# The low part of the weight tiles in block 0: from GpSimd to VectorE

## The chip, the cores and the metric

One core of a Trainium2 chip. The metric is device time in microseconds (us) of one execution of the whole program, median of three runs: 2673.79 us for the kernel before (2673.79 to 2675.59).

## The reference, cut to what matters

One layer of a recurrent decoder with two branches that read the same normalised input: a gated linear recurrence (LRU) and a gated delta rule (GDN). 2048 prompt tokens and 8 x 8 sample tokens go through it, in float32:

```python
u = rms_norm(x, norm_pre)
z = einsum('btd,de->bte', u, w_in)            # 1024 x 8208
# z -> lru_x, lru_gate, q|k|v, gdn_gate, b, a, m_lru, m_gdn
lru_out = rg_lru(conv(lru_x)) * silu(lru_gate)
gdn_out = norm(gated_delta_rule(conv+silu(q|k|v), g, beta)) * silu(gdn_gate)
merged  = sigmoid(m_lru) * (lru_out @ w_br_lru) + sigmoid(m_gdn) * (gdn_out @ w_br_gdn)
x_new   = x + rms_norm(merged @ w_out, norm_post)
```

Every weight matrix is used for every token. There are also the states of both branches as outputs.

## The kernel before, in words

**Precision by splitting.** TensorE works on a rounded float32 type. Each operand of a large product is therefore kept as two tiles, hi (the value rounded) and lo (the value minus hi), and a product is three matmuls: hi by hi, hi by lo and lo by hi (lines 551, 553 and 555 in `proj`). `split` (line 203) makes such a pair: ScalarE writes hi with a copy (it is recorded under line 143, as everything that goes through the ordered ScalarE wrapper), and another engine subtracts (line 205). Which engine that is, is the last argument of `split`: GpSimd where none is given.

**Blocks.** The 2048 prompt tokens are worked in four blocks of 512; block 0 also carries the 64 sample tokens, so its products have 576 columns (a half of 256 and a half of 320). A block goes through the same steps: normalised input (`u_tile`), then eight heads' k projections with their Gram matrices and a batched triangular inverse (`t_gram`, `t_inv`), the LRU groups (`t_lru`), then for each head the q, v and gate projections with the recurrent chain (`t_q`, `t_v`, `t_samp`, `t_chain`), then the two branch products (`branch`) and the output product (line 1294 on).

**Weights.** They are used in a fixed order (`worder`), 88 tiles of 128 x 1024 for a block. In block 0 each tile is read raw from the inputs by SyncE's queue (`wload`, lines 260 to 271), split into hi and lo in one tile `whl` (`wfetch`, line 296), and the pair is written to a DRAM scratch `dW` (`wstore`, line 279). In blocks 1 to 3 the pair is read back from there (line 300) and no split is done. `whl` has three buffers, the raw tiles two or three. `wfetch` runs one tile ahead of its use, a raw tile is loaded one or two tiles before that, and a tile's store is handed to SyncE's queue one tile later than its split. So a buffer of `whl` comes free when its matmuls have read it and its store has landed; a raw buffer comes free when both halves of the split have read it, and the next raw load on SyncE's queue waits for that.

**Who sets the order.** TensorE runs in the order of the program text, in which `Weave` mixes small tasks into the long projections. On the other engines the framework orders the instructions by their place in the text and their readiness in its own schedule; each engine then works strictly in that order and waits at an instruction whose inputs are late. On ScalarE a wrapper (`Ordered`) makes every later ScalarE instruction of a projection follow the hi of the tile that was fetched just before.

**The line that is changed.** In `wfetch`, `out` is true for the eight tiles of the output weight (their raw tile is `rawo`), which are split by ScalarE and VectorE already; the other 80 tiles of block 0 (raw tiles `raw` and `raws`) are split by ScalarE and GpSimd:

```python
wlast[0] = split(hi, lo, wraws[key(e)], V if out else None)
```

VectorE's other work in block 0 that the prediction speaks of: the convolution (lines 582 and 588, whose two tensor inputs both lie in SBUF), the elementwise part of SiLU (597), the inverse (816 to 826), the chain (1061, 1072, 1076), and the lo halves of activations (`xl` in `t_lru`, `bt` in the branch stage).

Of the kernel before, what the change touches and what calls it, by code (L numbers as in the profile page):

```python
# [154 lines left out]
def body(ctx, tc, x_prompt, x_sample, state_lru_conv, state_lru_h, state_gdn_conv, state_gdn_S,  # L155
# [5 lines left out]
    V, T, SP = nc.vector, nc.tensor, nc.sync  # L161
# [41 lines left out]
    def split(hi, lo, src, eng=None):  # L203
        r = A.activation(hi, src, AF.Copy)
        (eng or G).tensor_tensor(out=lo, in0=src, in1=hi.bitcast(F32), op=OP.subtract)  # L205
        return r
# [28 lines left out]
    key = lambda e: (e[0].tensor.name, e[1])  # L235
# [4 lines left out]
    wstores, wraws = [], {}  # L240

    wready = []
    wlast = [None]
# [3 lines left out]
    def wtile():  # L247
        ring[0] += 1
        if wx and ring[0] % 4 == 0:
            return wx[0].tile([128, 2, 1024], F32R, name="whx", tag="whx")  # L250
        return wp.tile([128, 2, 1024], F32R, name="whl", tag="whl", bufs=3)

    def wload(n):

        src, c = e = worder[n]
        if key(e) in wraws:
            return
        if isinstance(c, tuple):
            raw = rw.tile([128, 4, 256], F32, name="rawo", tag="raws")
            SP.dma_start(raw, src[c[1] * 512:(c[1] + 1) * 512, c[0] * 256:(c[0] + 1) * 256]  # L260
                         .rearrange("(k p) c -> p k c", p=128))
            wraws[key(e)] = raw
        elif not (paired[0] <= n < paired[1] or paired[2] <= n < paired[3]):
            raw = rw.tile([128, 8, 128], F32, name="raws", tag="raws")
            SP.dma_start(raw, src[:, c:c + 128].rearrange("(k p) c -> p k c", p=128))
            wraws[key(e)] = raw
        else:
            two = [key(x) for x in worder[n:n + 7]].count((src.tensor.name, c + 128))
            w = 128 + 128 * two
            raw = rp[0].tile([128, 8, w], F32, name="raw", tag="raw")  # L270
            SP.dma_start(raw, src[:, c:c + w].rearrange("(k p) c -> p k c", p=128))
            for j in range(1 + two):
                wraws[src.tensor.name, c + 128 * j] = raw[:, :, 128 * j:128 * j + 128]

    def wstore(held=0):

        while len(wstores) > held:
            i, hl = wstores.pop(0)
            SP.dma_start(dW[i], hl.bitcast(F32))

    def wfetch(ahead):

        while wnext[0] < len(worder) and len(wready) < ahead:
            n = wnext[0]
            e = worder[n]
            place = wplace[key(e)]
            out = isinstance(e[1], tuple)
            hl = wtile()
            hi, lo = (hl[:, j].rearrange("p (k c) -> p k c", c=256 if out else 128) for j in range(2))
            if n < len(wplace):  # L290
                while lnext[0] < len(wplace) and lnext[0] <= n + (
                        2 if paired[0] <= lnext[0] < paired[1] else 1):
                    wload(lnext[0])
                    lnext[0] += 1
                wstore(1)
                wlast[0] = split(hi, lo, wraws[key(e)], V if out else None)
                wstores.append((place, hl))
            else:
                wstore()
                SP.dma_start(hl.bitcast(F32), dW[place])  # L300
            wready.append((hi, lo))
            wnext[0] += 1

    def nextw():
        wfetch(1)
        w = wready.pop(0)
        return w
# [104 lines left out]
    with tc.tile_pool(name="init", bufs=2, side="right") as ip:  # L412
        with tc.tile_pool(name="u0", bufs=1) as up:
            r0 = ip.tile([8, 128], F32, name="r0")
            SP.dma_start(r0, rows(norm_pre))
            xh = u_load(0, up)
            t = gtile()
            tr(t[:, :8], r0, ident[:8, :8])
            V.tensor_copy(npre, t[:, :8])
            wraw = ip.tile([128, 8, 16], F32, name="wraw", bufs=1)  # L420
            SP.dma_start(wraw, win[:, C_B:C_B + 16].rearrange("(k p) c -> p k c", p=128))
            u_norm(xh, up)
            for n in range(2):
                wload(n)
                lnext[0] += 1
            SP.dma_start(dtb, bass.AP(tensor=gdn_dt_bias.tensor, offset=gdn_dt_bias.offset, ap=[[0, 128], [1, 8]]))
            SP.dma_start(negA, bass.AP(tensor=gdn_A_log.tensor, offset=gdn_A_log.offset, ap=[[0, 128], [1, 8]]))
            u = [u_tile(xh, k) for k in range(8)]
            zz = ip.tile([128, 96], F32, name="zz", bufs=1)
            V.memset(zz, 0.0)  # L430
            V.tensor_copy(wst[:, 256:352], zz)
            V.tensor_copy(wst3[:, :, 0:16], wraw)
            V.tensor_tensor(out=wst3[:, :, 16:32], in0=wraw, in1=wst3[:, :, 0:16].bitcast(F32), op=OP.subtract)
            wfetch(2)
# [96 lines left out]
    for blkno in range(NBLK):  # L531
# [9 lines left out]
        def proj(mov, evac):  # L541
            w = nextw()
            wfetch(3 if blkno else 1)
            A.after = wlast[0]
            hi, lo = w
            for c0, n in halves:
                ps = pmm.tile([128, 512], F32, name="mm", tag="mm")
                for k in range(8):
                    mh, ml = mov[k]
                    wh = hi[:, k, :]  # L550
                    T.matmul(ps[:, :n], wh, mh[:, c0:c0 + n], start=k == 0, stop=False)  # L551
                    W.pump(n * 0.4219)
                    T.matmul(ps[:, :n], wh, ml[:, c0:c0 + n], start=False, stop=False)  # L553
                    W.pump(n * 0.4219)
                    T.matmul(ps[:, :n], lo[:, k, :], mh[:, c0:c0 + n], start=False, stop=k == 7)  # L555
                    if k < 7:
                        W.pump(n * 0.4219)
                evac(ps, c0, n)
                W.pump(n * 0.4219)
# [654 lines left out]
        for k in range(8):  # L1214
            hi = pA.tile([128, TB + NS], F32R, name="a", tag="a")
            lo = pA.tile([128, TB + NS], F32R, name="a", tag="a")
# [20 lines left out]
        for dd in range(8):  # L1237
# [5 lines left out]
            hi = Bp.tile([128, NB], F32R, name="bt", tag="bt")  # L1243
            lo = Bp.tile([128, NB], F32R, name="bt", tag="bt")
# [108 lines left out]
```

## Time and profile before

| | before |
|---|---|
| median of three runs | 2673.79 us |
| the profiled execution | 2683.59 us, of which its span is 2681.9 us |
| TensorE busy (matmul) | 2571.7 us, 96% |
| VectorE busy | 1503.4 us, 56% |
| ScalarE busy | 885.4 us, 33% |
| GpSimd busy | 565.8 us, 21% |
| DMA | 581.82 MB, mean 217 GB/s |

The span runs from the first to the last instruction; the rest of the profiled execution lies around it. Busy shares are over the whole span. Block 0 ends near 886 us of it, the other three blocks take some 599 us each. In the rows PE is TensorE, DVE VectorE, ACT ScalarE, POOL GpSimd, SP SyncE; L205 is line 205; a name with q is an engine's queue. PEclk is the share of full clock that TensorE was granted.

### The profile page before, as it was taken

What the parts mean: (1) busy time and instruction counts of PE and PEld (TensorE: products, weight loads), DVE (VectorE), ACT (ScalarE), POOL (GpSimd) and SP (SyncE); (2) the same over time, 40 slices, a digit from 0 to 9 for tenths busy, and PEclk for the clock granted to TensorE, in tenths of its full rate; (3) what the DMA queues carried; (4) which work ended last, traced back from release to release, by engine and by line L of the source; (5) the groups of instructions that cost most, each with busy time, mean ns of one, the idle gap of its engine ahead of it and who ended that gap; (6) DMA issues with size and microseconds to landing.
All of it is one profiled execution on the core that took longest, in us unless ns stands there. A gap on an engine that the chain in (4) does not pass through costs nothing.

```text
span 2681.9 us, 39950 instructions
## 1 busy us (share of the span) xinstructions
PE 2571.7 (96%) x15332; PEld 2237.5 (83%) x15332; DVE 1503.4 (56%) x3441; ACT 885.4 (33%) x1722; POOL 565.8 (21%) x444
## 2 busy tenths in 40 slices
PE   6888799999999999999999999999999999999999
PEld 5887798888999788888889888888889888888888
DVE  4668477787434557566522557566513458566512
ACT  5324543333324225333302235333303235333301
POOL 2442342232540211100120121110210211110200
PEclk9988899999999999999999999999999999999999
DMA  7987978789887887554466787544466887555465
GB/s 190 250 257 187 228 207 187 203 176 179 255 292 256 283 277 222 200 177 158 154 237 256 260 283 225 203 163 163 154 245 256 270 272 217 200 172 168 160 236 200
DMA packets 327897, 581.82 MB, mean 217 GB/s; under 512 B 70849, under 2 KB 236762, under 8 KB 282650
## 3 DMA queue, kind: packets, MB, share of 16 engines
q1 hardware_dynamic: 313882, 553.57, 66.9%
q10 hardware_dynamic: 13824, 25.70, 2.5%
q8 instruction: 121, 1.98, 0.3%
q14 instruction: 70, 0.57, 0.1%
HBM read 421.61 MB, written 157.59 MB: 216 GB/s over the span
## 4 chain that ended last, share of the span: by engine, by line
PE 68%; DMA 3%; issue 2%; DVE 1%; POOL 1%; ACT 1%; SPq 0%; ACTq 0%; POOLq 0%; DVEq 0%
PE mm L555 17%; PE mm L551 16%; PE mm L553 16%; PE g L192 5%; PE c L192 4%; PE mm L1294 2%; PE mm L1298 2%; PE mm L1296 2%; PE g L196 2%; DMA er<-dgc 1%; DMA dgc<-gr 0%; DMA npb<-in_norm_post_dram 0%; DMA ux<-in_x_prompt_dram 0%; DMA whl<-dW 0%; POOL er L756 0%
## 5 line engine op out<-in xcount | busy, mean ns | idle before, releaser
L551 PE MATMUL mm<-a,whl 128*128 128x512 f32 (+2 forms) x2432 | 865.0, 356 | 25.2 <-ACT tmo L143 18.5
L555 PE MATMUL mm<-a,whl 128*128 128x512 f32 (+2 forms) x2432 | 869.6, 358 | 4.8 <-POOL whl L205 4.8
L553 PE MATMUL mm<-a,whl 128*128 128x512 f32 (+2 forms) x2432 | 863.9, 355 | 0.0
L551 PEld LDWEIGHTS mm<-a,whl 128*128 128x128 f32 x2432 | 466.7, 192 | 74.7 <-ACT tmo L143 20.0
L555 PEld LDWEIGHTS mm<-a,whl 128*128 128x128 f32 x2432 | 466.7, 192 | 58.0 <-POOL whl L205 5.4
L553 PEld LDWEIGHTS mm<-a,whl 128*128 128x128 f32 x2432 | 466.7, 192 | 45.6
L582 DVE SCALAR_TENSOR_TENSOR cvy<-cvr,cwg,cvy 128x512 f32<-128x512 f32 x288 | 224.7, 780 | 17.8 <-ACT cvy L143 12.4
L553 PE MATMUL mm<-a,whx 128*128 128x512 f32 x448 | 181.7, 406 | 0.0
L555 PE MATMUL mm<-a,whx 128*128 128x512 f32 x448 | 181.4, 405 | 0.0
L551 PE MATMUL mm<-a,whx 128*128 128x512 f32 x448 | 179.3, 400 | 0.0
L1232 DVE SCALAR_TENSOR_TENSOR pt<-tm,mm 128x512 f32<-128x512 f32 (+1 forms) x80 | 47.4, 592 | 189.8 <-PE mm L555 189.8
L143 ACT ACTIVATE cvr<-mm 128x512 f32<-128x512 f32 (+1 forms) x160 | 81.7, 510 | 175.4 <-PE mm L555 167.3
L1086 POOL TENSOR_TENSOR st<-st,mhalf 128x4 f32<-128x4 f32 x32 | 32.3, 1009 | 507.8 <-DVE st L1084 496.0
L205 POOL TENSOR_TENSOR whl<-raw,whl 128x1024 fp32r<-128x1024 f32 x44 | 108.8, 2474 | 118.4 <-ACT whl L143 108.6
L205 POOL TENSOR_TENSOR whl<-raws,whl 128x1024 fp32r<-128x1024 f32 x36 | 89.8, 2495 | 188.6 <-ACT whl L143 176.5
L1296 PE MATMUL mm<-whl,bt 128*128 128x256 f32 x448 | 126.4, 282 | 0.8 <-DVE whl L205 0.8
L1294 PE MATMUL mm<-whl,bt 128*128 128x256 f32 x448 | 126.2, 282 | 0.8 <-DVE y L1303 0.8
L1298 PE MATMUL mm<-whl,bt 128*128 128x256 f32 x448 | 126.2, 282 | 0.6 <-DVE yss L1272 0.6
L143 ACT ACTIVATE th<-cvy 128x512 f32<-128x512 f32 (+1 forms) x96 | 61.9, 644 | 195.7 <-DVE cvy L582 128.6
L143 ACT ACTIVATE yv<-c 128x128 f32<-128x128 f32 x128 | 35.5, 278 | 243.7 <-PE c L192 243.2
L555 PE MATMUL mm<-gp,whl 128*128 128x512 f32 (+2 forms) x296 | 104.2, 352 | 0.0
L551 PE MATMUL mm<-gp,whl 128*128 128x512 f32 (+2 forms) x296 | 104.1, 352 | 0.0
(341 smaller groups left out, 4637.8 us busy)
## 6 DMA issues: line engine op xcount, KB each, us to landing
whl<-dW SPq DMA_DIRECT2D x199, 1024.0 KB
dW<-whl SPq DMA_DIRECT2D x88, 1024.0 KB
whx<-dW SPq DMA_DIRECT2D x65, 1024.0 KB
raws<-in_w_in_dram SPq DMA_DIRECT2D x33, 512.0 KB
raw<-in_w_in_dram SPq DMA_DIRECT2D x15, 1024.0 KB
dtm<-tmo ACTq DMA_DIRECT2D x48, 256.0 KB
tm<-dtm SPq DMA_DIRECT2D x48, 256.0 KB
ux<-in_x_prompt_dram SPq DMA_DIRECT2D x16, 512.0 KB
```

The costliest lines, as they stand in the source:

```text
L143: r = f(*args, **kw)
L192: T.matmul(out, a, b, start=start, stop=stop)
L196: T.transpose(out, in_, idn)
L205: (eng or G).tensor_tensor(out=lo, in0=src, in1=hi.bitcast(F32), op=OP.subtract)
L551: T.matmul(ps[:, :n], wh, mh[:, c0:c0 + n], start=k == 0, stop=False)
L553: T.matmul(ps[:, :n], wh, ml[:, c0:c0 + n], start=False, stop=False)
L555: T.matmul(ps[:, :n], lo[:, k, :], mh[:, c0:c0 + n], start=False, stop=k == 7)
L582: V.scalar_tensor_tensor(out=y[:, :TB], in0=raw[:, i:i + TB], scalar=cw[:, i, ti:ti + 1], in1=y[:, :TB], op0=OP.mult, op1=OP.add)
L1232: proj(mov, lambda ps, c0, n: V.scalar_tensor_tensor(out=t_[:, c0:c0 + n], in0=x[:, c0:c0 + n], scalar=1.0, in1=ps[:, :n], op0=OP.add, op1 ...
L1294: T.matmul(ps[:, :256], mh[:, cs], wh[:, k % 4], start=k == 0, stop=False)
L1296: T.matmul(ps[:, :256], mh[:, cs], wl[:, k % 4], start=False, stop=False)
L1298: T.matmul(ps[:, :256], ml[:, cs], wh[:, k % 4], start=False, stop=k == 7)
```

## The change

The subtraction that makes lo of a weight tile goes to VectorE for all 88 tiles of block 0. Nothing else is edited.

```diff
@@ wfetch @@
                 wstore(1)
-                wlast[0] = split(hi, lo, wraws[key(e)], V if out else None)
+                wlast[0] = split(hi, lo, wraws[key(e)], V)
                 wstores.append((place, hl))
```

## Rows read from the trace of the kernel before

**Rows 1.** Busy time by stretch of block 0 (us, engines, PEclk, DMA).

```profile
core 0: us, PE busy (x) PEld busy (x) DVE busy (x) ACT busy (x) POOL busy (x), PEclk, DMA share, GB/s
0.00:75.00 75.00, 49.76 (x314) 43.42 (x315) 34.87 (x112) 39.07 (x83) 20.28 (x24) 1.00 0.74 198
75.00:220.00 145.00, 122.34 (x836) 117.74 (x836) 89.18 (x247) 45.03 (x92) 64.19 (x48) 0.93 0.88 245
220.00:312.00 92.00, 65.65 (x407) 64.23 (x407) 65.93 (x171) 46.55 (x81) 28.74 (x18) 0.82 0.84 206
312.00:411.00 99.00, 93.55 (x685) 90.69 (x684) 69.34 (x140) 48.05 (x86) 40.43 (x23) 0.95 0.84 224
411.00:700.00 289.00, 272.46 (x2012) 242.62 (x2012) 219.19 (x526) 98.72 (x230) 82.24 (x47) 1.00 0.84 181
700.00:803.00 103.00, 103.00 (x778) 103.00 (x777) 35.07 (x46) 28.22 (x36) 60.22 (x31) 1.00 0.82 300
```

**Rows 2.** Waits of PE, 0 to 886 us (total us, times, longest).

```profile
PE mm L551 <- ACT tmo L143: 18.5, 6, 7.3
...
PE g L196 <- DVE cvy L597: 9.4, 7, 1.4
PE c L192 <- DVE S L1072: 6.8, 7, 1.3
...
PE mm L555 <- POOL whl L205: 4.8, 2, 2.9
```

**Rows 3.** Instructions of line 205 (ns min/median/max, first and last start us, forms).

```profile
L205 POOL TENSOR_TENSOR whl<-raw,whl x44: 2340/2400/3160, 61.6 to 799.0; 128x1024 fp32r<-128x1024 f32 x44
L205 POOL TENSOR_TENSOR whl<-raws,whl x36: 2351/2412/2762, 20.7 to 719.7; 128x1024 fp32r<-128x1024 f32 x36
...
L205 DVE TENSOR_TENSOR whl<-rawo,whl x8: 1224/1225/1227, 804.6 to 865.0; 128x1024 fp32r<-128x1024 f32 x8
```

**Rows 4.** GpSimd's timeline at 68 us (start us, us, engine line op).

```profile
68.40 2.78 POOL L205 TENSOR_TENSOR whl<-raw,whl 128x1024 fp32r<-128x1024 f32 x1 [4.38 <-ACT whl L143]
```

**Rows 5.** VectorE's timeline around the split at 68.40 us.

```profile
68.16 0.75 DVE L582 SCALAR_TENSOR_TENSOR cvy<-cvr,cwg,cvy 128x512 f32<-128x512 f32 x1
68.82 2.44 DVE L588 SCALAR_TENSOR_TENSOR cvy<-cvs,cwg,cvy 128x64 f32<-128x64 f32 x1
```

**Rows 6.** Instructions of line 588 (ns min/median/max).

```profile
L588 DVE SCALAR_TENSOR_TENSOR cvy<-cvs,cwg,cvy x72: 265/274/2440, 53.8 to 667.5; 128x64 f32<-128x64 f32 x72
```

**Rows 7.** VectorE's timeline: first and last of its lengthened instructions.

```profile
54.00 2.90 DVE L582 SCALAR_TENSOR_TENSOR cvy<-cvr,cwg,cvy 128x512 f32<-128x512 f32 x1
...
799.80 2.21 DVE L205 TENSOR_TENSOR bt<-pt,bt 128x576 fp32r<-128x576 f32 x1 [2.26 <-ACT bt L143]
```

**Rows 8.** Timeline of one head: VectorE's instructions.

```profile
498.78 2.40 DVE L588 SCALAR_TENSOR_TENSOR cvy<-cvs,cwg,cvy 128x64 f32<-128x64 f32 x1
...
502.40 0.33 DVE L1072 SCALAR_TENSOR_TENSOR S<-S,egl,c 128x128 f32<-128x128 f32 x1
...
510.25 2.43 DVE L588 SCALAR_TENSOR_TENSOR cvy<-cvs,cwg,cvy 128x64 f32<-128x64 f32 x1
...
516.21 0.75 DVE L597 SCALAR_TENSOR_TENSOR cvy<-th,cvy 128x576 f32<-128x576 f32 x1
```

**Rows 9.** The same head: TensorE's wait before the transposes.

```profile
517.01 0.44 PE L196 MATMUL g<-ident,cvy 128*128 128x128 f32 x2 [1.35 <-DVE cvy L597]
```

**Rows 10.** VectorE in the inverse, 220 to 261 us.

```profile
244.12 2.66 DVE L823 TENSOR_TENSOR invT<-invT,invt 128x231 f32<-128x231 f32 x1
```

**Rows 11.** SyncE's queue in the same stretch.

```profile
260.94 0.31 SPq L848 DMA_DIRECT2D dD<-invT  x1
...
269.99 0.34 SPq L279 DMA_DIRECT2D dW<-whl  x1
```

**Rows 12.** Waits of SyncE's queue, 0 to 886 us.

```profile
SPq L265 <- POOL whl L205: 113.8, 26, 11.2
```

**Rows 13.** SyncE's queue: the third raw load.

```profile
23.06 0.40 SPq L265 DMA_DIRECT2D raws<-in_w_in_dram  x1
```

**Rows 14.** Waits of all engines, 0 to 886 us.

```profile
POOL whl L205 <- ACT whl L143: 285.1, 52, 16.8
...
ACT whl L143 <- DMA dW<-whl: 52.7, 12, 8.8
...
DVE xl L205 <- ACT xh L143: 7.9, 4, 6.7
```

## The prediction

> **What bounds the kernel now.** I first read the busy time by stretch, because the change touches block 0 alone. In the last stretch before the output product, 700 to 803 us, TensorE is busy for the whole 103 us; between 75 and 700 us it is not, and the gaps are largest from 220 to 312 us, where it works 65.65 of 92 us and is granted 0.82 of its clock [rows 1]. Subtracting busy from length, TensorE stands still for 22.7, 26.4, 5.5 and 16.5 us in the four stretches from 75 to 700 us. Three of them also run below full clock: the lost clock is 145 x 0.07 + 92 x 0.18 + 99 x 0.05 = 32 us of time at full speed. Every such low stretch follows gaps, so a us of gap removed there is worth more than a us.
>
> Then the waits: TensorE rarely waits for a weight's lo itself (4.8 us, twice). What it waits for most is ScalarE's evacuation of the matrices (18.5 us) and, in the stage of the heads, two VectorE results, 9.4 and 6.8 us in seven waits each [rows 2]. So what the change does to VectorE's queue decides, not what it does to GpSimd's.
>
> Third, VectorE's timeline beside GpSimd's. A GpSimd subtraction of a weight takes 2.40 us [rows 3]. One starts at 68.40 us and ends at 71.18; the small convolution step of line 588, put to VectorE at 68.82, ends at 71.26 [rows 4, 5]. That step has a median of 0.274 us [rows 6]; here it took 2.44. The pattern repeats: between the first, at 54.00 us, and the last, at 799.80 us [rows 7], I count 55 VectorE instructions that lie over a GpSimd weight split and last more than 0.4 us longer than their kind ordinarily does; together they lose 101 us. By stretch they lose 6.5, 19.9, 14.1, 20.7, 30.0 and 10.1 us (the stretches of rows 1 in order). GpSimd is thus not the free helper that its 21% of busy time suggests: each of its subtractions may hold VectorE for up to its own length.
>
> **The change, step by step.**
>
> Removed: 80 GpSimd subtractions, 44 + 36 [rows 3], some 198 us of GpSimd time that nothing waits for directly but 4.8 us. With them go up to 101 us of lengthened VectorE instructions.
>
> Added: 80 VectorE subtractions. The eight output weights already do this in the same shape: 1.225 us, within 3 ns [rows 3]. 80 x 1.225 = 98 us. By stretch there are 6, 14, 9, 12, 23 and 16 tiles, that is 7.4, 17.2, 11.0, 14.7, 28.2 and 19.6 us. So VectorE's balance from 75 to 700 us is -2.7, -3.1, -6.0 and -1.8 us: about even. The gain cannot come from less VectorE time, only from where it falls and from lo being there earlier.
>
> *Heads (411 to 700 us).* Each head has three weight tiles; two GpSimd splits land on line 588. At 498.78 one costs 2.40 us instead of 0.27; VectorE is then busy without a break until the state update at 502.40, for which TensorE waits. At 510.25 the other costs 2.43 us; VectorE stays near full until SiLU at 516.21 [rows 8], and TensorE waits 1.35 us for that [rows 9]. ScalarE's hi ends just ahead of both places, so I expect lo there: 1.2 us in place of a loss of 2.15 us, VectorE 0.95 us earlier. Over seven heads that takes 0.95 us from each 1.35 us wait and all of the other: 6.7 + 6.8 = 13.5 us. The third tile's lo falls where VectorE is dense and costs 1.2 us; the lead of 0.95 covers all but 0.25, x 7 = 1.8. Net -11.5 us. If the cover is not there, the three lo cost 3.7 us a head.
>
> *LRU and inverse (220 to 312 us).* VectorE is full here, and the inverse's stores are issued from 260.94 us on; a weight store, behind them in SyncE's queue, leaves at 269.99 [rows 11]. One of the inverse's steps, 0.4 us of work, took 2.66 us under a split [rows 10]. VectorE's balance of -3.1 us comes out at SyncE's queue. I take 3 us of gap, with 0.63 us of lost clock to each (16.6 us lost clock for 26.4 us of gap): -5 us.
>
> *75 to 220 and 312 to 411 us.* In the first, DMA is busy 0.88 of the time [rows 1] and the gaps stem from stores and loads behind one another; lo comes 1.2 us sooner, and SyncE's raw loads, which stand 113.8 us waiting for GpSimd's lo [rows 12], leave sooner by as much. Most of that wait is for hi, since GpSimd itself waits 285.1 us for it [rows 14]. I take -2 us. In the second only 5.5 us are idle; -2 us.
>
> *Start.* The third raw load leaves at 23.06 us when the first lo is done [rows 13], and TensorE's input transposes later stand behind it on ScalarE: -1 us.
>
> *700 to 803 us.* VectorE gains 19.6 us of work and loses 10.1 us of delay, with 35.07 us of 103 busy [rows 1]. TensorE's own work hides it: 0. If that cover fails, 9.5 us at most.
>
> *The new wait.* lo now stands in VectorE's ordered queue, and behind it stand the convolutions, SiLU and the chain, for which ScalarE and TensorE wait. When hi is late, VectorE stops there. hi waits 52.7 us in twelve waits for a buffer's store to land [rows 14]. No row shows a weight's lo on VectorE in these stretches. The lower bound is nothing: in those waits ScalarE stands too, and most of VectorE's inputs come from it. The upper bound is the 52.7 us. The nearest row is the activation split `xl`, also hi on ScalarE and lo on VectorE: four of eight wait, 7.9 us in all [rows 14]. That is 1 us each; for twelve late ones 12 us of VectorE, of which I let 4 reach TensorE.
>
> *The other side of the holding.* Other GpSimd work remains, 296 - 198 = 98 us of the 803 us [rows 1, 3], or 12%. A lo that meets it waits about half a us: 80 x 0.12 x 0.5 = 5 us of VectorE, 1 us of it on the path.
> The Trainium skill, "SBUF — State Buffer", section "Who interferes with whom", says that VectorE's instructions with two SBUF inputs and GpSimd's reads take one shared port pair in turn, whole instruction by whole instruction, whichever came first. The pair of rows at 68 us agrees; taken alone, the rule speaks against this change as well, since the subtraction on VectorE has two SBUF inputs, and it would make the 1 us above up to 5.
>
> Sum: -11.5 - 5 - 2 - 2 - 1 + 4 + 1 = -16.5 us. The profiled execution of before took 2683.59 us, 9.8 us above the median shown and 1.7 us above its span; so 2667 us for it, and 2673.8 - 16.5 = 2657 us for the median.
>
> **The rivals.**
>
> *VectorE stands in line for ScalarE (slower).* The place is 75 to 312 us, where hi is late. For it: the 52.7 us of late hi, and that gaps here also cost clock. Against it: ScalarE stands at the same moments. If the late hi cost TensorE through VectorE as much again as the 18.5 us it now waits for ScalarE, plus 0.63 of clock, that is +30 us; the gain outside the heads is gone, the heads keep 11.5. Result: 2692 us. It decides as soon as more than some 17 us of late hi reach TensorE.
>
> *Nothing that can be measured.* The gaps before 411 us belong to DMA and SyncE, and in the heads the third lo eats what the first two give. For it: VectorE's balance is nearly even, DMA is busy 0.84 to 0.88. Against it: the waits of the heads follow VectorE's backlog so regularly. 2670 to 2676 us. The framework may also order VectorE's work otherwise, so that lo does not fall where the split fell; that ends here or in the first rival.
>
> **Chances.** Forecast 0.58; VectorE in line 0.25; nothing 0.17. Faster by over 0.2% (5.3 us, about what a measurement of this kernel tells from no change): 0.58; within it 0.17; slower 0.25. Range: at the low end the heads give all 16.2 us of their two waits and the stretches from 75 to 411 us a quarter of their 54.6 us of gaps and 32 us of clock, 22: 2635. At the high end the first rival, 2692. The forecast's own range is 2635 to 2668.
>
> **What would show it.** Line 588 has no instruction near 2.4 us under a weight split any more; VectorE's busy time in 411 to 700 us stays within 5 us of 219; the two seven-fold waits of the heads shrink below 8 us together; the inverse's first store leaves before 260 us. Wrong it would be if VectorE's waits for ScalarE's `whl` sum to over 20 us before 312 us and TensorE's gaps there grow, or if the heads' period does not fall by about 1.6 us.

## The result, and the profile after

The changed kernel takes 2662.53 us (median of four runs, 2656.97 to 2665.83) against 2674.68 us of before, measured beside it: ratio 0.9941, 95% interval 0.9925 to 0.9957, or 12 us faster. The forecast was 2657 us, in a range of 2635 to 2692. Measured again later beside other kernels, where before stood at 2679.95 us, the change took 2670.30 us: ratio 0.9960, 0.9944 to 0.9976. So it is worth some 10 to 12 us. The profiled execution after took 2665.83 us with a span of 2664.1 us, 17.8 us less than the span of before; as the profiled execution of before lay 9.8 us above its median and that of after only 3.3 us above its own, part of that difference is not the change.

The busy time by stretch, after (columns as in [rows 1]):

```profile
75.00:220.00 145.00, 126.77 (x894) 123.36 (x893) 92.66 (x281) 50.31 (x101) 33.14 (x35) 0.95 0.92 259
220.00:312.00 92.00, 73.57 (x495) 72.14 (x495) 66.33 (x186) 54.09 (x94) 8.13 (x9) 0.91 0.92 219
312.00:411.00 99.00, 90.99 (x672) 85.96 (x671) 68.93 (x162) 41.13 (x79) 10.86 (x10) 0.95 0.80 211
411.00:700.00 289.00, 274.45 (x2029) 247.55 (x2029) 216.38 (x525) 104.56 (x233) 41.71 (x31) 0.99 0.81 189
700.00:803.00 103.00, 102.76 (x778) 102.56 (x777) 48.19 (x68) 29.26 (x37) 14.99 (x12) 1.00 0.83 301
```

VectorE (third number) has 80 instructions more and is hardly busier before the branches: 66.33 us against 65.93 from 220 to 312 us, 216.38 against 219.19 in the heads; only from 700 to 803 us does it work 13 us more. GpSimd has lost its 80 instructions. TensorE works 4.4 us more of the 145 us from 75 on, 7.9 us more of the next 92, at a granted clock of 0.91 in place of 0.82.

The reason that VectorE is hardly busier stands in two views of after, the instructions of line 588 and of line 205 (ns min/median/max, first and last start):

```profile
L588 DVE SCALAR_TENSOR_TENSOR cvy<-cvs,cwg,cvy x72: 266/278/729, 54.1 to 646.9; 128x64 f32<-128x64 f32 x72
```

```profile
L205 DVE TENSOR_TENSOR whl<-raw,whl x44: 1199/1225/2064, 60.1 to 778.8; 128x1024 fp32r<-128x1024 f32 x44
L205 DVE TENSOR_TENSOR whl<-raws,whl x36: 1156/1218/2503, 19.4 to 698.2; 128x1024 fp32r<-128x1024 f32 x36
```

The longest small convolution step took 0.73 us; before it was 2.44 [rows 6]. Counted as in the prediction, the 101 us of VectorE's lengthening under weight splits are gone, and about 25 us under GpSimd's other work are left. (Such counts, here and below, move by about a tenth with what is taken as an instruction's ordinary time.) The lo's themselves meet that work: their medians are about the 1.225 us of [rows 3], the longest took 2.5 us.

Where did the time go? TensorE's order is the same in both kernels, so the same matmul, counted from the start (15332 in each trace), can be looked up in both. The place of before is in us; the others are differences to it in us, from one profile each. Matmuls 1148, 1553 and 2236 are those that before reaches at 220, 312 and 411 us, where the prediction's stretches end.

| matmul no. | stage | before | after | after, second profile |
|---|---|---|---|---|
| 300 | k stage, fifth tile | 73.4 | +0.3 | +0.6 |
| 900 | k stage, last tile | 175.9 | +0.8 | +1.7 |
| 1148 | LRU, the inverse begins | 220.1 | -7.3 | -3.3 |
| 1200 | LRU, beside the inverse | 237.8 | -18.1 | -14.1 |
| 1500 | LRU | 292.1 | -21.8 | -19.2 |
| 1553 | LRU | 312.1 | -24.4 | -21.3 |
| 2100 | first head | 388.7 | -14.5 | -10.3 |
| 2236 | second head begins | 411.2 | -18.8 | -14.4 |
| 2400 | second head | 435.9 | -20.3 | -15.9 |
| 3600 | before the seventh head's vt | 606.4 | -25.0 | -21.3 |
| 4200 | heads done | 694.1 | -19.3 | -12.8 |
| 5100 | branches done | 813.4 | -19.4 | -12.9 |

Nearly all of what is left at the end is won between 176 and 238 us, that is with the last tile of the k stage and the first five of the LRU stage. These 300 matmuls took 61.9 us before and 43.0 after: TensorE's gaps fell from 13.2 to 2.5 us, and its busy time from 48.9 to 40.6 us, at a granted clock of 1.00 in place of 0.86. The heads win about a us each up to the sixth, and lose it all in the seventh. The two profiles of the changed kernel differ by up to 6.5 us, so a few us between single profiles tell little.

### The profile page after: what moved, and what is told of

Read it like the earlier page. It is cut to its first block, busy times and chain, and to the rows that moved or that the text cites. A ratio compares the mean times of both kernels' runs of the same rounds, so it can differ in the third digit from the quotient of the medians.

```text
span 2664.1 us, 39927 instructions
## 1 busy us (share of the span) xinstructions
PE 2564.3 (96%) x15332; PEld 2232.2 (84%) x15332; DVE 1508.0 (57%) x3521; ACT 886.9 (33%) x1722; POOL 378.0 (14%) x364
## 4 chain that ended last, share of the span: by engine, by line
PE 77%; DMA 10%; DVE 6%; issue 2%; ACT 2%; SPq 1%; POOL 1%; ACTq 0%; POOLq 0%; DVEq 0%
PE mm L555 18%; PE mm L553 18%; PE mm L551 18%; PE g L192 8%; PE c L192 5%; PE g L196 2%; PE mm L1294 2%; PE mm L1296 2%; PE mm L1298 2%; DMA er<-dgc 2%; DMA raws<-in_w_in_dram 2%; DMA dW<-whl 2%; DVE cvy L582 1%; DVE whl L205 1%; DMA dE<-er 1%
## 5 line engine op out<-in xcount | busy, mean ns | idle before, releaser
L582 DVE SCALAR_TENSOR_TENSOR cvy<-cvr,cwg,cvy 128x512 f32<-128x512 f32 x288 | 217.4, 755 | 17.9 <-ACT cvy L143 12.5
L1086 POOL TENSOR_TENSOR st<-st,mhalf 128x4 f32<-128x4 f32 x32 | 38.9, 1215 | 653.4 <-DVE st L1084 653.4
L143 ACT ACTIVATE th<-cvy 128x512 f32<-128x512 f32 (+1 forms) x96 | 61.9, 645 | 156.4 <-DVE cvy L582 130.9
L555 PE MATMUL mm<-gp,whl 128*128 128x512 f32 (+2 forms) x296 | 104.2, 352 | 0.0
L551 PE MATMUL mm<-gp,whl 128*128 128x512 f32 (+2 forms) x296 | 104.1, 352 | 0.0
L553 PE MATMUL mm<-gp,whl 128*128 128x512 f32 (+2 forms) x296 | 104.0, 351 | 0.0
L551 PEld LDWEIGHTS mm<-a,whx 128*128 128x128 f32 x448 | 84.5, 189 | 17.6
```

What stands on the lines that cost most here:

```text
L143: r = f(*args, **kw)
L582: V.scalar_tensor_tensor(out=y[:, :TB], in0=raw[:, i:i + TB], scalar=cw[:, i, ti:ti + 1], in1=y[:, :TB], op0=OP.mult, op1=OP.add)
L1086: G.tensor_tensor(out=st[:, 3], in0=st[:, 2], in1=mhalf[:, :NCH], op=OP.pow)
```

## The gain from the k stage to the LRU stage, and what it is made of

The timeline of before at the place where the gain is made (start us, us, engine line op):

```profile
181.17 2.21 DVE L584 COPY halog<-cvr 128x3 f32<-128x3 f32 x1 [3.92 <-ACT cvr L143]
...
184.94 2.88 DVE L582 SCALAR_TENSOR_TENSOR cvy<-cvr,cwg,cvy 128x512 f32<-128x512 f32 x1
...
190.05 0.76 DVE L597 SCALAR_TENSOR_TENSOR kT<-th,cvy 128x576 f32<-128x576 f32 x1
...
189.33 0.68 ACT L143 ACTIVATE th<-cvy 128x576 f32<-128x576 f32 x1 [5.30 <-DVE cvy L588]
...
190.34 0.64 PE L551 MATMUL mm<-a,whl 128*128 128x320 f32 x1 [4.04 <-ACT tmo L143]
```

Two instructions of the convolution, 0.16 and 0.74 us of work, are held for 2.1 us each. ScalarE, which works in order, stands 5.30 us for the convolution; the evacuation of the next projection stands behind, and TensorE waits 4.04 us for it. In the timeline of after the same SiLU product follows a lo and comes 7.7 us sooner:

```profile
181.26 1.21 DVE L205 TENSOR_TENSOR whl<-raw,whl 128x1024 fp32r<-128x1024 f32 x1
182.39 0.74 DVE L597 SCALAR_TENSOR_TENSOR kT<-th,cvy 128x576 f32<-128x576 f32 x1
```

The same is seen 50 us later, beside the inverse:

```profile
233.31 2.53 DVE L823 TENSOR_TENSOR invT<-invT,invt 128x240 f32<-128x240 f32 x1
...
236.21 0.75 DVE L205 TENSOR_TENSOR xl<-cvy,xh 128x576 fp32r<-128x576 f32 x1
...
237.01 0.39 PE L192 MATMUL g<-xl,gwh 128*128 128x256 f32 x1 [3.12 <-DVE xl L205]
```

A step of 0.42 us is held for 2.1, `xl` stands behind it, and TensorE waits 3.12 us for `xl`.

Three readings were to be told apart. Theory 1: GpSimd's subtraction holds VectorE. Theory 2: lo is there sooner, for TensorE and for SyncE's queue. Theory 3: another order of the queues, which any edit may give.

**One stage at a time.**

```diff
-wlast[0] = split(hi, lo, wraws[key(e)], V)
+wlast[0] = split(hi, lo, wraws[key(e)], V if out or n < 35 else G)         # k and LRU alone
+wlast[0] = split(hi, lo, wraws[key(e)], V if out or 35 <= n < 64 else G)   # heads alone
```

> Only the 35 tiles of the k and LRU stages have lo on VectorE; heads and branches stay on GpSimd. The trace after shows TensorE 19 us earlier at the end of these stages, nearly all of it between 176 and 220 us. Theory 1 (the hold on VectorE in the k and LRU stages) and theory 2 (lo sooner, SyncE's queue freed sooner) both expect most of the gain: 2655 to 2665 us. Theory 3 (the 18 us come from another order of the queues, which any edit of the schedule may give or take): the sum of this gain and of the heads' alone misses the whole gain by more than 6 us.

> Only the 29 tiles of the stage of the heads (and the eight output tiles, as before) have lo on VectorE; the other 51 stay on GpSimd. Theory 1 (GpSimd's subtraction holds VectorE, and the gain comes where that hold stood ahead of a wait of TensorE): the heads' period falls from 38.3 to 37.1 us as with the whole change, some 8 us less: 2664 to 2669 us. Theory 2 (the gain comes from lo being there sooner for SyncE's queue, in the stages before the heads): within 3 us of before, 2672 to 2677 us.

The k and LRU tiles alone: 2661.58 us against 2679.73 of before, ratio 0.9929 (0.9916 to 0.9943); measured again 2661.78, 0.9935. The heads alone: 2685.81 us, ratio 1.0027 (1.0016 to 1.0037), slower. 18.2 us won and 6.1 lost make 12.1, the gain of the whole change, so the 6 us of disagreement that theory 3 wants do not show; the intervals of the two are some 3 us either way. The kernels with lo on VectorE in these stages reach matmul 1200 between 12 and 18 us sooner, whatever else was edited, but for the next one, with 9.3; heads alone reaches it 0.4 us later. The profile of the heads alone, its fastest run, does not show the loss of 6.1 us: it is 2.2 us ahead of before when the heads are done. Where the loss arises is open. Both theories expected the heads wrongly; that is taken up below.

**The hold without the lateness.** The change, and GpSimd reads each hi of 32 tiles again:

```diff
 wlast[0] = split(hi, lo, wraws[key(e)], V)
+if 2 <= n < 34:
+    scr = klp[0].tile([128, 3, 128], F32, name="scr", tag="scr", bufs=1)
+    for a, m in ((0, 3), (3, 3), (6, 2)):
+        G.tensor_tensor(out=scr[:, :m], in0=bc(ones[:, None, :], [128, m, 128]),
+                        in1=hi[:, a:a + m].bitcast(F32), op=OP.subtract)
```

> The change as it is (lo on VectorE, as soon as there), and beside it for 32 tiles of the k and LRU stages GpSimd reads the same hi again in three instructions (ones minus hi, into a scratch tile that nothing uses): the hold without the lateness. Theory 1: VectorE's instructions are lengthened again, by 20 to 40 us in these stages, on top of the subtractions that it now does; a third to all of the gain of 18 us there goes: 6 to 20 us above the change (12 us below before would become 6 below to 8 above). Theory 2: as the change, within 4 us of it.

2681.48 us, ratio 1.0005 (0.9996 to 1.0013): the gain is gone. Some 80 VectorE instructions are lengthened under the added reads, by 54 us. TensorE is 9.3 us ahead of before at matmul 1200 and 2.2 at 2100, where the change is 18.1 and 14.5 ahead. lo was still made by VectorE, yet it now came late too, since VectorE was held; TensorE's waits from 75 to 411 us (total us, times, longest; line 561 is line 555 of the change):

```profile
PE mm L557 <- ACT tmo L143: 17.6, 5, 6.3
PE mm L561 <- DVE whl L205: 12.4, 4, 4.8
```

So moving lo gains no time while GpSimd goes on reading, as theory 1 expected. By itself this run does not part it from theory 2, since lo was late: from the tenth to the twentieth weight tile it ended 3.8 us after its hi on average, where before took 2.9 and the change 2.2. Two runs below part them. With VectorE's work doubled, lo was hardly sooner than before (2.8 us after its hi) and GpSimd subtracted no weight; TensorE was 13.2 us ahead at matmul 1200. With zeros, lo was there before its hi; the lead there, 15.4 us, is no larger than the change's 14 to 18. So the lead does not come from a sooner lo. Of what the hold carries, the added reads show the larger part: at matmul 2236, as the second head begins, the change is 18.8 and 14.4 us ahead, zeros 22.1, and with GpSimd reading again it is 6.8. In this profile some lead is left, though the time shows none; what carries that rest is not shown.

A fourth reading, that GpSimd's other work comes sooner once the subtractions are gone, finds no support: ScalarE's waits for GpSimd's `er`, the longest for that work, sum to 31.7 us in seven waits from 75 to 411 us before, and to 30.4 in eight after.

**The hold cut into pieces.** As before, with GpSimd's subtraction in four; the cut shows the branch for the 80 tiles.

```diff
+raw = wraws[key(e)]
+wlast[0] = A.activation(hi, raw, AF.Copy)
+for j in range(0, 8, 2):
+    G.tensor_tensor(out=lo[:, j:j + 2], in0=raw[:, j:j + 2],
+                    in1=hi[:, j:j + 2].bitcast(F32), op=OP.subtract)
```

> All 80 subtractions stay on GpSimd as before, but each is cut into four of 256 columns (0.72 us or more each by the gate weights' subtraction of that size, so some 3.0 us in place of 2.4). lo is thus later than before by 0.6 us, and VectorE gets no work. Theory 1 (GpSimd holds VectorE for one instruction's length): a VectorE instruction that meets one waits 0.8 us at most in place of 2.4; the lengthening falls from 101 to some 50 us, and the time is 6 to 20 us below before of the same call. Theory 2 (what helps is lo being there sooner, for TensorE and SyncE's queue): no gain or a loss, 0 to 10 us above before.

2684.84 us, ratio 1.0017 (1.0009 to 1.0026). This run tells nothing between the theories, because its premise failed: the pieces take 263 us of GpSimd in place of 199, they lengthen some 160 VectorE instructions where the whole ones lengthened 55, and the sum nearly stays, 85 to 90 us against 101. A likely reason, not tested, is that the next small instruction meets the next piece. Lengthening nearly unchanged and time unchanged agree, no more.

**No reading and no VectorE work.** GpSimd fills lo with zeros; the subtraction of 80 tiles is left out (the cut shows their branch).

```diff
+wlast[0] = A.activation(hi, wraws[key(e)], AF.Copy)
+G.memset(lo.bitcast(F32), 0.0)
```

> Leaves out the subtraction of the 80 tiles: GpSimd fills lo with zeros, which reads nothing, and VectorE gets no work. If a GpSimd instruction that only writes does not hold VectorE, no VectorE instruction is lengthened under a fill. Theory 1: VectorE has neither the 101 us of holds nor the 98 us of subtractions, so the heads' waits vanish and the time is below the change by another 5 to 15 us: 2647 to 2658 us. Theory 2: lo is there about as soon as with the change (the fill of 1088 columns took 1.0 us), so the time is that of the change, 2659 to 2667 us.

2647.37 us, ratio 0.9878 (0.9860 to 0.9896), at the low end of theory 1's range; by the ratios it is 17 to 22 us below the change, where theory 1 asked for 5 to 15 and theory 2 for none. Only some 17 VectorE instructions are lengthened under fills, by 10 us, most of them copies with one input. This bounds the case: had neither engine to subtract, 32 us would be won, of which the change takes 10 to 12. The 20 us between are what VectorE's 98 us of new work and its later lo cost together; this run does not part the two.

**VectorE's work doubled.** (`scr` is an added tile of 128 x 8.)

```diff
 wlast[0] = split(hi, lo, wraws[key(e)], V)
+if not out:
+    V.tensor_reduce(out=scr, in_=hi.bitcast(F32), axis=AX.X, op=OP.add)
```

> The change, and VectorE also sums each hi of the 80 tiles along 1024 columns into a scratch tile that nothing uses: the added VectorE time doubled (about another 1.1 to 1.2 us a tile, 90 us in all), lo no later for TensorE than one such instruction. If VectorE's added time lies on the path wherever it is dense (heads, inverse), the heads lose up to 3.6 us each and the inverse 10 us: 20 to 45 us above the change. If other work hides it: within 5 us of the change.

2675.32 us, ratio 0.9986 (0.9978 to 0.9995), 5 us above the second measurement of the change and 13 above the first: between the two prices asked. Its trace says where: from matmul 1200 to 1500, the stage of the inverse, its lead shrinks from 13.1 to 4.0 us; through the heads, where the same load came three times a head, the lead stays (5.5 us at 2400, 5.3 at 4200). In this profile VectorE's time is on the path at the inverse, and hidden in the heads.

## The heads: a gain that one late tile takes back

The timeline of after in an ordinary head:

```profile
478.60 1.21 DVE L205 TENSOR_TENSOR whl<-raws,whl 128x1024 fp32r<-128x1024 f32 x1
479.73 0.75 DVE L597 SCALAR_TENSOR_TENSOR qT<-th,cvy 128x576 f32<-128x576 f32 x1
480.40 0.34 DVE L1072 SCALAR_TENSOR_TENSOR S<-S,egl,c 128x128 f32<-128x128 f32 x1
...
490.25 1.22 DVE L205 TENSOR_TENSOR whl<-raws,whl 128x1024 fp32r<-128x1024 f32 x1
491.38 0.75 DVE L597 SCALAR_TENSOR_TENSOR cvy<-th,cvy 128x576 f32<-128x576 f32 x1
...
493.88 1.22 DVE L205 TENSOR_TENSOR whl<-raws,whl 128x1024 fp32r<-128x1024 f32 x1
...
480.79 0.49 PE L192 MATMUL c<-S,kT 128*128 128x128 f32 x2 [0.46 <-DVE S L1072]
...
495.75 0.33 PE L196 MATMUL g<-ident,kq 128*128 128x128 f32 x1 [0.64 <-DVE vt L1041]
```

It is as forecast in kind. Two lo's take the place of the two holds of [rows 8], and TensorE's waits of 0.94 and 1.35 us become 0.46 and 0.64. The second is now for vt, which stands behind the third lo. The state wait recurs at 517.9 us: the period is 37.1 us, by the same two waits of before 38.3.

At the vt of the seventh head this happens (same view, ScalarE, VectorE, TensorE, SyncE; it is the sixth of TensorE's seven waits for vt from 411 us on, and the expectations below say sixth head for it):

```profile
610.83 1.06 ACT L143 ACTIVATE whl<-raws 128x1024 fp32r<-128x1024 f32 x1 [6.81 <-DMA raws<-in_w_in_dram]
...
611.92 1.23 DVE L205 TENSOR_TENSOR whl<-raws,whl 128x1024 fp32r<-128x1024 f32 x1 [6.66 <-ACT whl L143]
613.06 0.68 DVE L1041 TENSOR_TENSOR vt<-g,wk 128x512 f32<-128x512 f32 x1
...
613.80 0.47 PE L196 MATMUL g<-ident,kq 128*128 128x128 f32 x1 [7.39 <-DVE vt L1041]
...
596.27 0.37 SPq L1107 DMA_DIRECT2D Sall<-in_state_gdn_S_dram  x1
596.73 0.53 SPq L265 DMA_DIRECT2D raws<-in_w_in_dram  x1
```

A raw tile is late, ScalarE's hi waits 6.81 us for it, VectorE stands 6.66 us at lo with vt behind it, and TensorE stands 7.39 us. The clock records grant half from 610.95 us on, for 6.8 us. Before, TensorE has no such wait in this stage. This is the prediction's first rival, at another place than it named.

**The change again, and the queue ahead of the raw load.** The raw load stood behind the load of the sample state (line 1107), which waits for the store of the head before out of the same buffer. Waits of SyncE's queue, 0 to 886 us, after (before: 5.8 us, twice):

```profile
SPq L1107 <- DMA out_dram<-Sall: 25.5, 7, 6.8
```

With lo on VectorE, the framework puts that load ahead of the raw load in SyncE's order; before it came behind. One run repeats the change, one moves that load to GpSimd's queue:

```diff
-SP.dma_start(Sall, state_gdn_S[0, :, h].rearrange("b k v -> k b v"))
+G.dma_start(Sall, state_gdn_S[0, :, h].rearrange("b k v -> k b v"))
```

> The change again, beside the two below on the same chip: ratio 0.992 to 0.996, as the first measurement had it; its trace shows once more one wait of some 7 us for vt in the sixth head if that is of the program's order, and none or another place if it is chance.

> The change, with the load of the sample state (line 1107) issued from GpSimd's queue in place of SyncE's, where it waits for the store of the head before and stands ahead of the raw weight load. Theory (the late hi in the sixth head comes from that place in SyncE's queue): the 7 us wait for vt goes, raw loads no longer wait behind it, 5 to 12 us below the change: 2650 to 2658 us where the change has 2662. Rival (DMA itself is late there): the wait stays, same time within 4 us. Against both: GpSimd's own small powers of the chain now wait behind the load, up to 3 us a head slower.

> lo on VectorE for the 35 tiles of the k and LRU stages alone, again: if the heads give nothing net (period shorter by 1.2 us, one late hi of 7 us with its lost clock), it stands 0 to 5 us below the change in the same call; if the heads give, 3 to 8 us above it.

TensorE's waits for vt from 411 to 700 us, first in the repeated change, then with the load moved:

```profile
PE g L196 <- DVE vt L1041: 13.2, 7, 9.6
```

```profile
PE g L196 <- DVE vt L1041: 9.2, 7, 5.3
```

In the repeated change (ratio 0.9960) the long wait is in the same head, 9.6 us, and with the heads alone it is there too, 8.2 us; so it belongs to the program, not to chance. With the load moved it is 5.3 us, and the time 2661.23 us, ratio 0.9929 (0.9914 to 0.9945): 9 us below the change measured beside it. The wait is not all of that: the profile with the load moved was already 8.4 us ahead of the repeated change at matmul 2400, before this wait. The raw load and the hi that waits for it, with the load moved:

```profile
586.59 3.11 SPq L265 DMA_DIRECT2D raws<-in_w_in_dram  x1
...
604.21 1.06 ACT L143 ACTIVATE whl<-raws 128x1024 fp32r<-128x1024 f32 x1 [4.76 <-DMA raws<-in_w_in_dram]
```

In after the buffer of this raw tile came free at 591.11 us and the load was issued at 596.73; with the load of the sample state moved, it was issued as its buffer came free. So the place in the queue cost 5.6 us and is a part of the cause. But hi then began 17.6 us after the issue, where after took 14.1 and before at most 16.4. That the raw load is that slow there is thus the other part. Why, with SyncE's issues taking 3 to 4 us each around 600 us, is left open. The k and LRU tiles alone, in this measurement 8.5 us below the change, beat its expectation of at most 5.

**The third tile back on GpSimd.** From this the third tile of each head looked better on GpSimd.

```diff
+third = 35 <= n < 59 and (n - 35) % 3 == 2
+wlast[0] = split(hi, lo, wraws[key(e)], G if third else V)
```

> As after the change, but the third tile of each head, whose subtraction on GpSimd held no VectorE instruction, goes back to GpSimd (8 tiles). Theory 1: VectorE's backlog ahead of the transposes of v goes, TensorE's waits for vt (0.64 us a head, and 7.4 us once) go: 5 to 12 us below the change, 2650 to 2658 us. Rival (a third subtraction on GpSimd, now met by other VectorE work, holds it again): no better than the change, 2660 to 2668 us.

2671.76 us, ratio 0.9965 (0.9952 to 0.9978): no better, the rival's case. Seven VectorE instructions are now held by it, 12 us in all; before, that tile's subtraction had held one instruction in each of the first two heads and none in the other six. TensorE's waits for vt in the heads grew from 0.64 to 1.68 us (line 1042 is line 1041 there):

```profile
PE g L196 <- DVE vt L1042: 8.9, 6, 1.7
```

**Pieces in the heads.** k and LRU tiles on VectorE, heads and branches on GpSimd in four pieces.

> lo on VectorE for the 35 tiles of the k and LRU stages (as in the run with those alone, ratio 0.9929), and on GpSimd in four pieces for heads and branches. Theory 1: the heads lose most of their two waits without VectorE's added time and without lo standing in VectorE's line behind a late hi: 4 to 12 us below that run, ratio 0.988 to 0.992. Rival (a hold in pieces meets more instructions and costs as much): ratio 0.992 to 0.995.

2670.21 us, ratio 0.9962 (0.9948 to 0.9976), above both ranges, though its interval touches the rival's. Some 75 VectorE instructions were lengthened by 40 us; the lead over before stays at 15 us through the heads. The pieces give nothing, as in the run with pieces alone. It starts the heads 5 us later than the run without pieces, although the two kernels are the same up to there; two profiles of the change differ there by 4.4 us.

Zeros show what the heads could give: there TensorE's lead grows from 23.9 us at matmul 2400 to 37.4 at 4200, and the only wait left in the stage is this:

```profile
PE g L192 <- DMA Sall<-in_state_gdn_S_dram: 3.3, 1, 3.3
```

## Why the prediction was right, and where it was not

The direction and the mechanism, a hold that goes with GpSimd's subtraction, were right, and the total came near: the sum was -16.5 us, measured were 10 to 12 us less. That it came near is luck. The heads were to give 11.5 us of it and gave next to nothing; the stretch from 220 to 312 us gave 17 us where 5 were taken. The figures below are from the table's rows 1148, 1553 and 2236 and, for 700 us, matmul 4246 (-19.4 and -12.9), first and second profile.

- **Removed and added VectorE time:** right. 101 us of lengthening went, 80 subtractions at 1.22 us came, and VectorE's busy time in the heads stayed within 3 us.
- **75 to 220 us, -2 us:** 7.7 and 4.0 us were won. I had put those gaps down to stores and loads, as DMA is busy 0.88 there [rows 1]. But ScalarE's 5.30 us stand for a held convolution, and the evacuation behind it, were in the waits that I had summed [rows 2]; I looked for holds ahead of TensorE's waits in the heads and not here.
- **LRU and inverse (220 to 312 us), -5 us:** the term that failed on the low side; 17.0 and 18.0 us were won. The same work took 92.0 us before and 74.9 after. TensorE's gaps fell by 11.1 us (26.4 to 15.3) where 3 were taken; the clock that came with each us of gap, 0.54 us, was near the 0.63 taken. I had looked for VectorE's balance at SyncE's queue alone. TensorE's waits for `xl`, for hi and for the evacuation, 3.1, 2.9 and 3.5 us there, are gone; for `xl` the rows above show the hold in front of it, for the other two it is not shown. How this stretch's gain splits into causes stays open: with GpSimd reading again it is as large (18 us, but from a lead that is 5 to 9 us smaller at its start), with zeros only 7. At SyncE's queue the term was right: the inverse's first store leaves at 257.73 us, 3.2 us sooner than in [rows 11]:

```profile
257.73 0.33 SPq L848 DMA_DIRECT2D dD<-invT  x1
```

- **312 to 411 us, -2 us:** 5.6 and 6.9 us were lost. TensorE now waits 6.8 and 6.4 us for the inverse's blocks from DRAM (Dn; 1.4 us before): it is some 20 us ahead there, and the inverse's store only 3.2.
- **Heads, -11.5 us:** the step that failed. The two waits shrank by 0.48 and 0.71 us a head, 1.2 together, where 1.9 less 0.25 were taken. That gave 6 to 7 us up to the seventh head. Then the late tile takes back 7.4 us (9.6 in the second profile) and its clock. Net 0.6 us won and 1.5 lost, where 11.5 were to be won (the term's own parts make 11.7), and with the heads alone the time is 6 us longer.
- **The new wait, +4 us, at most 52.7 of VectorE:** its bound was too low. VectorE waited 88.3 us in 40 waits for a weight's hi (waits of all engines, after, 0 to 886 us):

```profile
DVE whl L205 <- ACT whl L143: 88.3, 40, 9.2
```

I had counted hi that waits for a buffer; hi that waits for its raw tile, or stands in ScalarE's line behind other work, counts too. TensorE felt one of these as a wait of 7.4 us, in the seventh head. It also waits for lo itself (waits of TensorE, after, 0 to 886 us):

```profile
PE mm L555 <- DVE whl L205: 7.3, 5, 2.8
```

That was 4.8 us in two waits before [rows 2]. I had taken lo as 1.2 us sooner throughout. In the k stage it ends 0.9 us sooner after its hi; in the LRU stage 1.0 us later (3.9 us after its hi on average, 3.0 before), because there it stands in VectorE's order behind steps of the inverse: the hi of one tile ends at 215.8 us, its lo begins at 223.51.

The rule that I gave for being wrong (over 20 us of such waits before 312 us, with TensorE's gaps growing) was half met: 59.8 us in 15 waits, but the gaps shrank. In 43.9 of these 59.8 us ScalarE stood as well, as the lower bound had it.
- **Start -1, branches 0, other holds +1:** +0.3, 0, and 13 us by which lo's were lengthened where 5 were estimated; six of these are lo's of the branch stage that met GpSimd's additions, under TensorE's own work.

Of the rivals, *VectorE in line for ScalarE* is real and decides the heads, but not the sum. *Nothing* was close: with 5 us in place of 17 and 18 from 220 to 312 us, the two profiles would end 7 us ahead and level with before.

Of the signs that were named, line 588, VectorE's time in the heads and the inverse's store came as said. The two waits of the heads sum to 14.5 us, not to less than 8, because one of them now holds the late tile's 7.4; and the period fell by 1.2 us where 1.6 was named.

On the rule of "SBUF — State Buffer" (the Trainium skill, section "Who interferes with whom"): the runs agree that GpSimd's reading holds VectorE for an instruction's length, and that a fill holds far less (10 us under 80 fills). It also bears on the change itself, as the prediction weighed: lo on VectorE was held by GpSimd's remaining work and took up to 2.5 us.

## What to carry to other kernels

An engine that looks idle is not a free helper when its reads hold a busier one. Look for instructions that take a multiple of their kind's median, ending when the helper's instruction ends, and follow them to the next wait of the bounding engine; do so in every stage, not only where the pattern is regular. When an instruction moves into a queue that others depend on, ask when its input can be late and what stands behind it: here the best kernels that still subtract move only the tiles of the first stages (0.993), or move all and take the load that made one tile late out of the way (0.993); both stood 8 to 9 us below the change measured beside them.

## What the runs showed of the hardware that was not expected

Cutting GpSimd's subtraction into four hardly shortened what it cost VectorE: some 160 lengthened instructions of about 0.55 us each in place of 55 of 1.8. And even copies of 128x3 elements were held: 2.21 us at 181.17 us in before, where their kind takes 0.16.
